# Stated queue orders for ScalarE and VectorE, and four block-product pairs instead of three in three input projections, in a one-core transformer layer

## Chip, cores and metric

The kernel runs on one core of a Trainium2 chip. The metric is the device time of one execution in microseconds (us); the median of the runs is compared. TensorE (PE) multiplies, VectorE (DVE) and ScalarE (ACT) prepare weights and evacuate results, GpSimd (POOL) issues a few accumulating transfers, SyncE (SP) issues the weight loads.

## The reference

One layer of a hybrid decoder, sequence 256, width 2048, all in fp32:

```python
x = x + 0.5 * swiglu(rmsnorm(x), w_gate1, w_up1, w_down1)     # FFN 1, hidden width 5632
h = rmsnorm(x)
q, k, v, mq, mk, mv, mo, mi, mf = split(h @ w_in)             # one input projection, 7176 columns
y_a = diff_attention(q, k, v)                                  # 4 heads
y_b = mlstm(silu(conv(mq, mk)), mv, mi, mf) * sigmoid(mo)      # 4 heads
x = x + concat(y_a, y_b) @ w_out
x = x + 0.5 * swiglu(rmsnorm(x), w_gate2, w_up2, w_down2)     # FFN 2
out = rmsnorm(x)
```

## The kernel before

**Products.** The 256 rows of x are two halves of 128; an output chunk is 512 columns (`CW`) and one half, one accumulator bank. Each fp32 weight tile is split into a high part (`wh`, a ScalarE copy, L116) and a low remainder (`wl`, a VectorE subtraction, L117); the activations are held in the same form (`xt`, `xs`). A product is then three matmuls of 128x512: high by high (L146), low of x by high (L147), high of x by low (L149, issued after the others of its unit). A unit is two K tiles of 128.

**Block products.** `Paired` computes two output chunks (columns of `wa` and of `wb`) at once. For the first `ns` of the pairs of K tiles it uses 7 block products instead of 8 (21 matmuls instead of 24 for such a pair); the rest is done as plain units. `first()` loads a pair of both weights (`raw`), forms weight sums on VectorE (L388 `sums<-raw`, L390 `raw<-sums,raw`), splits sums and weights (`halves_of`), and accumulates p5, p7 (`p57`) and p1, p6 (`p16`); after `p16` a GpSimd transfer adds one block of `raw` to another (L409, `raw<-raw`). `combine()` merges the banks: u is copied from p1 (ACT L434), u += p6 (DVE L435), p7 += u (L436), u3 copied from p7 (ACT L437), p6 = p5 - u3 (L438), p5 -= u (L439). `second()` adds to p1, p7, p5 the products of the bare weights (`bare`, which needs the transfer of L409), of the upper right block (`upper`), and the plain units of `wa`; `third()` adds the plain units of `wb`.

**Stages.** `Chain.run` interleaves `first()` of one `Paired` with `third()` of the one before. An FFN runs 11 gate and up pairs with `ns` = 4 of 8 (`NP`), in groups of 3, 3, 3, 2, each group followed by its share of the two down projections with `ns` = 3, 3, 3, 1 (`NP_DOWN`); the last, with `ns` = 1, ends an FFN. The mixer's five input projections use `ns` = 3 (`NP_MIX`), the out projection 2. At the start of FFN 1 `load_xt` loads and splits x, and `sum_xt` makes the sum form of a pair of x (`xg`, `xsum`, `xs`).

**What sets the order.** Each engine runs its own queue in order. The program is a list of tile operations with priorities (`high_priority`): weight loads, sums and splits are put 400 places ahead of where they stand (`AHEAD`), evacuations under `soon()` 440. A scheduler turns this into the queues. Buffers that bound how far loads and splits run ahead: `raw` 4, `rawp` and `sums` together 5, `wh`/`wl` 4 pairs. SP issues the weight loads in order, each when its buffer is free.

## Time and profile before

| | |
|---|---|
| time, median of 3 runs (lowest to highest) | 1796.76 us (1793.56 to 1799.55) |
| profiled execution: its own time | 1798.07 us |
| its span | 1796.4 us |
| mean granted TensorE clock | 0.997 |
| PE busy | 1773.1 us (99%), 8033 instructions |
| DVE busy | 1566.1 us (87%) |
| ACT busy | 1163.8 us (65%) |
| POOL busy | 176.7 us (10%) |

The span is the time from the first to the last recorded work; the execution's own time lies 1.67 us above it. Busy is the sum of an engine's instruction times without overlaps; a wait is the idle time ahead of an instruction, with the event that ended it.

### The profile page before, as it was taken

The numbers are of one execution on the slowest core, as the hardware profiler recorded it, in microseconds if no ns is written. First come the engines' busy times: TensorE is split into PE (matmuls) and PEld (weight loads), VectorE is DVE, ScalarE is ACT, GpSimd is POOL, SyncE is SP. The second block draws the span as 40 slices with busy tenths as digits, with TensorE's granted clock in tenths as the row PEclk, the third lists the DMA queues.
The fourth block names the chain that finished last, engine by engine and source line by source line (L and its number), as shares of the span: only waits on it lengthen the run. The fifth ranks groups of instructions, "written<-read, shape, count | busy, mean of one in ns | idle before, by whom it ended". The sixth has DMA issues, their size and how long they took to land.

```text
span 1796.4 us, 23431 instructions
## 1 busy us (share of the span) xinstructions
PE 1773.1 (99%) x8033; PEld 1463.6 (81%) x8033; DVE 1566.1 (87%) x1895; ACT 1163.8 (65%) x1512; POOL 176.7 (10%) x220
## 2 busy tenths in 40 slices
PE   9999999999999999999999999999999999999998
PEld 6788888887888878987888888888888888888886
DVE  6988899988998877796787988999899988998886
ACT  6666666666666656676566766666666666666664
POOL 0001100111002100000000000001100111002100
PEclk9999999999999999999999999999999999999999
DMA  9777877887788863665656665778877788778864
GB/s 340 220 226 223 239 230 231 258 237 223 218 261 235 257 236 122 209 215 196 196 191 197 192 194 165 220 240 249 233 243 232 249 236 243 211 254 239 262 193 152
DMA packets 124649, 402.76 MB, mean 224 GB/s; under 512 B 14001, under 2 KB 14513, under 8 KB 124273
## 3 DMA queue, kind: packets, MB, share of 16 engines
q1 hardware_dynamic: 96192, 349.35, 56.6%
q0 software_dynamic: 27328, 49.82, 16.5%
q10 hardware_dynamic: 1008, 2.09, 0.3%
q8 instruction: 63, 1.03, 0.2%
q14 instruction: 58, 0.47, 0.1%
HBM read 349.56 MB, written 2.10 MB: 196 GB/s over the span
## 4 chain that ended last, share of the span: by engine, by line
PE 86%; DMA 5%; issue 4%; DVE 4%; ACT 1%; SPq 0%; POOL 0%; DVEq 0%; POOLq 0%; ACTq 0%
PE acc L146 28%; PE acc L149 27%; PE acc L147 27%; DVE wl L117 2%; DMA raw<-in_wu_dram 2%; DMA rawp<-in_wu_dram 2%; PE tr L307 1%; ACT wh L116 1%; DVE sums L388 1%; DMA raw<-raw 0%; PE tr L250 0%; PE sc L946 0%; SPq L173 0%; PE num L897 0%; PE tr L689 0%
## 5 line engine op out<-in xcount | busy, mean ns | idle before, releaser
L116 ACT CAST wh<-raw 128x1024 fp32r<-128x1024 f32 (+3 forms) x448 | 402.0, 906 | 282.6 <-PE acc L147 180.4
L146 PE MATMUL acc<-wh,xt 128*128 128x512 f32 (+3 forms) x1444 | 559.8, 389 | 3.1 <-ACT wh L116 3.0
L147 PE MATMUL acc<-wh,xt 128*128 128x512 f32 (+3 forms) x1444 | 557.0, 387 | 0.0
L117 DVE TENSOR_TENSOR wl<-raw,wh 128x1024 fp32r<-128x1024 f32 (+3 forms) x448 | 459.7, 1039 | 86.2 <-ACT wh L116 83.2
L116 ACT CAST wh<-rawp 128x1024 fp32r<-128x1024 f32 (+1 forms) x358 | 372.7, 1044 | 156.0 <-PE acc L147 133.3
L117 DVE TENSOR_TENSOR wl<-rawp,wh 128x1024 fp32r<-128x1024 f32 (+1 forms) x358 | 430.9, 1207 | 44.9 <-ACT wh L116 41.6
L146 PE MATMUL acc<-wh,xs 128*128 128x512 f32 (+2 forms) x1071 | 420.2, 393 | 6.7 <-ACT wh L116 2.9
L147 PE MATMUL acc<-wh,xs 128*128 128x512 f32 (+2 forms) x1071 | 414.8, 388 | 0.0
L149 PE MATMUL acc<-wl,xt 128*128 128x512 f32 (+3 forms) x1444 | 398.5, 386 | 0.4 <-DVE wl L117 0.4
L149 PE MATMUL acc<-wl,xs 128*128 128x512 f32 (+2 forms) x1071 | 335.9, 389 | 2.7 <-DVE wl L117 2.5
L146 PEld LDWEIGHTS acc<-wh,xt 128*128 128x128 f32 x1444 | 271.5, 188 | 60.6 <-ACT wh L116 5.8
L147 PEld LDWEIGHTS acc<-wh,xt 128*128 128x128 f32 x1444 | 271.6, 188 | 54.0
L149 PEld LDWEIGHTS acc<-wl,xt 128*128 128x128 f32 x1444 | 269.7, 188 | 54.7 <-DVE wl L117 0.8
L146 PEld LDWEIGHTS acc<-wh,xs 128*128 128x128 f32 x1071 | 201.5, 188 | 49.0 <-ACT wh L116 3.7
L149 PEld LDWEIGHTS acc<-wl,xs 128*128 128x128 f32 x1071 | 200.1, 188 | 47.3 <-DVE wl L117 6.9
L409 POOL DMA_DIRECT2D raw<-raw x141 | 121.5, 863 | 1187.8 <-DVE wl L117 852.4
L147 PEld LDWEIGHTS acc<-wh,xs 128*128 128x128 f32 x1071 | 201.5, 188 | 39.4 <-DVE xs L112 0.4
L388 DVE TENSOR_TENSOR sums<-raw 128x1024 f32<-128x1024 f32 x141 | 171.8, 1219 | 43.7 <-DMA raw<-in_wu_dram 38.9
L116 ACT CAST wh<-sums 128x1024 fp32r<-128x1024 f32 x141 | 148.5, 1053 | 83.7 <-PE acc L147 62.6
L117 DVE TENSOR_TENSOR wl<-sums,wh 128x1024 fp32r<-128x1024 f32 x141 | 171.8, 1219 | 12.5 <-ACT wh L116 10.1
L390 DVE TENSOR_TENSOR raw<-sums,raw 128x512 f32<-128x512 f32 x141 | 96.3, 683 | 0.8
L293 POOL DMA_DIRECT2D xres<-part x48 | 44.4, 1002 | 265.6 <-ACT part L292 264.4
(199 smaller groups left out, 804.4 us busy)
## 6 DMA issues: line engine op xcount, KB each, us to landing
rawp<-in_wd_dram SPq DMA_DIRECT2D x96, 512.0 KB, 5.6
rawp<-in_wu_dram SPq DMA_DIRECT2D x94, 512.0 KB, 7.5
raw<-in_wg_dram SPq DMA_DIRECT2D x89, 512.0 KB, 7.1
rawp<-in_wg_dram SPq DMA_DIRECT2D x86, 512.0 KB, 6.0
raw<-in_wu_dram SPq DMA_DIRECT2D x82, 512.0 KB, 7.8
raw<-in_wd_dram SPq DMA_DIRECT2D x80, 512.0 KB, 6.2
raw<-raw POOLq DMA_DIRECT2D x141, 256.0 KB, 6.2
rawp<-in_win_dram SPq DMA_DIRECT2D x50, 512.0 KB, 4.9
```

The lines of the kernel that those rows point to most:

```text
L116: nc.scalar.copy(hi, src)
L117: nc.vector.tensor_tensor(out=lo, in0=src, in1=hi.bitcast(F32), op=ALU.subtract)
L146: nc.tensor.matmul(acc, lh, rh, start=first, stop=False, skip_group_check=on)
L147: nc.tensor.matmul(acc, ll, rh, start=False, stop=False, skip_group_check=on)
L149: nc.tensor.matmul(acc, lh, rl, start=False, stop=last, skip_group_check=on)
L293: nc.gpsimd.dma_start(xres[:, hb, c * CW:(c + 1) * CW], t, accum_op=ALU.add)
L307: nc.tensor.transpose(tr[:, i, hb * P:(hb + 1) * P], hs[hb][:, k * P:(k + 1) * P], ident)
L388: nc.vector.tensor_tensor(out=sums[j], in0=raw[:, 0:4:3, :], in1=raw[:, 2:3, :].to_broadcast([P, 2, CW]), op=ALU.add)
L390: nc.vector.tensor_tensor(out=raw[:, 2, :], in0=sums[j][:, 0, :], in1=raw[:, 3, :], op=ALU.add)
L409: nc.gpsimd.dma_start(raw[:, 2, :], raw[:, 1, :], accum_op=ALU.add)
```

## The change

Five things are changed. The middle three of the five input projections use 4 pairs in block products instead of 3 (`NPS_MIX`), and the sum form of x is made for 4 pairs there. `after(late, early)` states an order between two instructions of one engine without a semaphore: evacuations (`add_part`, `gate`, `gated`, the copies and additions of `combine`) are stated ahead of weight splits that come 4 or more splits later (`SLACK`), and a sum (L388, now L413) behind the VectorE split that lies 4 back (`SUMS`). `combine` is cut in two: u and u += p6 right behind the last `p16`, the rest (`combine_rest`) at the end of `first()`. Where `ns == 1`, the plain unit comes before the block products, and their split behind the copy of u3. At the start, two pairs of x get their sum form in `load_xt`, and the explicit call in `ffn` is gone.

```diff
-NP_MIX = 3
+NP_MIX = 4
+NPS_MIX = (3,4,4,4,3)
...
+SLACK = 4
+SUMS = 4
...
     def split(src, hi, lo):
-        nc.scalar.copy(hi, src)
-        nc.vector.tensor_tensor(out=lo, in0=src, in1=hi.bitcast(F32), op=ALU.subtract)
+        return (nc.scalar.copy(hi, src),
+                nc.vector.tensor_tensor(out=lo, in0=src, in1=hi.bitcast(F32), op=ALU.subtract))
+    splits, queued = [], ([], [])
+    def after(late, early):
+        tc.add_manual_dep(late.ins, early.ins.name,
+                          mybir.DependencyInfo(mybir.DependencyClass.NoSync, mybir.DependencyReason.DATA),
+                          reason="order")
+    def ahead_of_splits(i, ins):
+        queued[i].append((len(splits), ins))
+    def split_weights(src, hi, lo):
+        made = split(src, hi, lo)
+        for late, q in zip(made, queued):
+            while q and len(splits) >= q[0][0] + SLACK:
+                after(late, q.pop(0)[1])
+        return made
...
         with soon():
-            nc.scalar.activation(s, src, AF.Silu, scale=r)
+            ahead_of_splits(0, nc.scalar.activation(s, src, AF.Silu, scale=r))
...
-                    nc.vector.tensor_tensor(out=sums[j], in0=raw[:, 0:4:3, :],
-                                            in1=raw[:, 2:3, :].to_broadcast([P, 2, CW]), op=ALU.add)
+                    made = nc.vector.tensor_tensor(out=sums[j], in0=raw[:, 0:4:3, :],
+                                                   in1=raw[:, 2:3, :].to_broadcast([P, 2, CW]), op=ALU.add)
+                    if len(splits) >= SUMS:
+                        after(made, splits[-SUMS][1])
...
             p16(0)
+            if last == 0:
+                self.combine()
...
                 p16(j)
+                if j == last:
+                    self.combine()
...
                     p57(j)
+            self.combine_rest()
             yield
...
         def combine(self):
+            self.u = wk("u")
             with soon():
+                ahead_of_splits(0, nc.scalar.copy(self.u, self.p1))
+                ahead_of_splits(1, nc.vector.tensor_tensor(out=self.u, in0=self.p6, in1=self.u, op=ALU.add))
+        def combine_rest(self):
+            u, u3 = self.u, wk("u3")
+            p5, p6, p7 = self.p5, self.p6, self.p7
+            with soon():
+                ahead_of_splits(1, nc.vector.tensor_tensor(out=p7, in0=p7, in1=u, op=ALU.add))
+                self.copied = nc.scalar.copy(u3, p7)
+                ahead_of_splits(0, self.copied)
                 nc.vector.tensor_tensor(out=p6, in0=p5, in1=u3, op=ALU.subtract)
                 nc.vector.tensor_tensor(out=p5, in0=p5, in1=u, op=ALU.subtract)
...
             def bare(j):
...
-                    split(self.raws[j][:, 1:3, :], *t)
+                    splits.append(split_weights(self.raws[j][:, 1:3, :], *t))
+                    if self.ns == 1:
+                        after(splits[-1][0], self.copied)
...
-                if i < self.ns:
-                    bare(i)
-                    if i % 2 or i == self.ns - 1:
-                        upper(i - i % 2)
+                def blocks():
+                    if i < self.ns:
+                        bare(i)
+                        if i % 2 or i == self.ns - 1:
+                            upper(i - i % 2)
+                if self.ns > 1:
+                    blocks()
                 if i < len(self.rest):
...
+                if self.ns == 1:
+                    blocks()
...
-            p.combine()
             self.end()
...
-                    first[1]()
                     chain.put(stream, NP, functools.partial(end, au))
...
-        if u == KD // UK - 1:
+        if u >= KD // UK - NP_FIRST:
             sum_xt()
...
-    def both(c):
-        return Paired(xp2, win[c], win[c + 1], KD, NP_MIX)
+    def both(c, ns):
+        return Paired(xp2, win[c], win[c + 1], KD, ns)
```

The queues are shown at three places. A number behind a name tells buffers apart. First, VectorE at the start of the fifth gate and up pair of FFN 1 (174 to 202 us of the trace), before: `sums_1752` is the first weight sum there, `wl_1766` the sixth split behind it.

```order
L388 TENSOR_TENSOR sums_1752<-raw_1749 128x1024
L117 TENSOR_TENSOR wl_1697<-rawp_1694,wh_1696 128x1024
L390 TENSOR_TENSOR raw_1749<-sums_1752,raw_1749 128x512
L388 TENSOR_TENSOR sums_1797<-raw_1794 128x1024
L117 TENSOR_TENSOR wl_1729<-sums_1725,wh_1728 128x1024
L117 TENSOR_TENSOR wl_1739<-raw_1722,wh_1738 128x1024
L117 TENSOR_TENSOR wl_1756<-sums_1752,wh_1755 128x1024
L390 TENSOR_TENSOR raw_1794<-sums_1797,raw_1794 128x512
L388 TENSOR_TENSOR sums_1824<-raw_1821 128x1024
L117 TENSOR_TENSOR wl_1766<-raw_1749,wh_1765 128x1024
```

And with the change (L413 is L388 of before, L417 is L390, L120 is L117):

```order
L413 TENSOR_TENSOR sums_1752<-raw_1749 128x1024
L120 TENSOR_TENSOR wl_1697<-rawp_1694,wh_1696 128x1024
L417 TENSOR_TENSOR raw_1749<-sums_1752,raw_1749 128x512
L120 TENSOR_TENSOR wl_1729<-sums_1725,wh_1728 128x1024
L120 TENSOR_TENSOR wl_1739<-raw_1722,wh_1738 128x1024
L120 TENSOR_TENSOR wl_1756<-sums_1752,wh_1755 128x1024
L413 TENSOR_TENSOR sums_1797<-raw_1794 128x1024
L120 TENSOR_TENSOR wl_1766<-raw_1749,wh_1765 128x1024
L417 TENSOR_TENSOR raw_1794<-sums_1797,raw_1794 128x512
L120 TENSOR_TENSOR wl_1779<-rawp_1776,wh_1778 128x1024
```

The sum `sums_1797` has moved from ahead of three splits to behind them, and `sums_1824` from ahead of `wl_1766` to behind it, with its own addition (L390, L417).

Second, ScalarE at the first down projection with `ns == 1` (655 to 671 us), before; `raw_5603` is the pair of the block products, `rawp_5729` the plain unit, `u_5702` and `u_1171_5703` the copies of p1 and p7:

```order
L116 CAST wh_5686<-rawp_5684 128x1024
L116 CAST wh_5712<-raw_5603 128x1024
L116 CAST wh_5722<-raw_5603 128x512
L434 COPY u_5702<-acc_5599 128x512
L116 CAST wh_5731<-rawp_5729 128x1024
L437 COPY u_1171_5703<-acc_5601 128x512
L116 CAST wh_5765<-rawp_5763 128x1024
```

And with the change (L119 is L116, L466 is L434, L474 is L437; `rawp_5712` is the plain unit, `u_5666` and `u_1165_5669` the copies):

```order
L119 CAST wh_5694<-rawp_5692 128x1024
L119 CAST wh_5714<-rawp_5712 128x1024
L466 COPY u_5666<-acc_5599 128x512
L474 COPY u_1165_5669<-acc_5601 128x512
L119 CAST wh_5730<-raw_5603 128x1024
L119 CAST wh_5740<-raw_5603 128x512
L119 CAST wh_5765<-rawp_5763 128x1024
```

The plain unit's copy and the two copies of p1 and p7 have moved ahead of the copies of `raw_5603`.

Third, ScalarE at the start of FFN 1, before; `wh_149` is the first weight tile, in two halves, `xs_132` and `xs_139` the first two K pairs of x:

```order
L116 CAST wh_149<-raw_145 128x512
L111 ACTIVATE xs_132<-xraw_130,prm 128x256 x2
L111 ACTIVATE xs_139<-xraw_130,prm 128x256
L116 CAST wh_149<-raw_145 128x512
L111 ACTIVATE xs_139<-xraw_130,prm 128x256
L116 CAST wh_167<-raw_145 128x1024
```

And with the change (L114 is L111, L369 is L344):

```order
L119 CAST wh_149<-raw_145 128x512
L114 ACTIVATE xs_132<-xraw_130,prm 128x256
L369 ACTIVATE xg_301<-xraw_130,prm 128x256 x2
L114 ACTIVATE xs_139<-xraw_130,prm 128x256
L119 CAST wh_149<-raw_145 128x512
L114 ACTIVATE xs_139<-xraw_130,prm 128x256
L114 ACTIVATE xs_132<-xraw_130,prm 128x256
L119 CAST wh_167<-raw_145 128x1024
```

One slice of `xs_132` has moved behind the second half of `wh_149` and the slice of `xs_139`, and the gained copy `xg_301` of a second pair has come in.

## Rows read from the trace of the kernel before

**Rows 1.** The page of the profiled execution: the span, and the busy time of each engine with its share and instructions.

```profile
span 1796.4 us, 23431 instructions
...
PE 1773.1 (99%) x8033; PEld 1463.6 (81%) x8033; DVE 1566.1 (87%) x1895; ACT 1163.8 (65%) x1512; POOL 176.7 (10%) x220
```

**Rows 2.** TensorE's waits over the whole span for weight tiles: instruction and tile, what it waited for, us in total, times, longest.

```profile
PE acc L146 <- ACT wh L116: 5.9, 7, 2.5
PE acc L149 <- DVE wl L117: 2.9, 7, 0.6
```

**Rows 3.** The chain of waits: start in us, us, what. One unstalled group of four matmuls, and a transfer in the gate and up products of FFN 1.

```profile
65.48 0.91 PE acc L149 x4
...
269.57 7.73 DMA rawp<-in_wu_dram
```

**Rows 4.** Busy time by stretch: the stretch, its length, busy us of PE, PEld, DVE, ACT, POOL (instructions), granted clock of TensorE, share of the DMA engines, GB/s. FFN 1 without its start and end, the end of FFN 1, and the mixer.

```profile
60.00:660.00 600.00, 596.46 (x2663) 492.04 (x2662) 540.45 (x594) 385.16 (x453) 68.21 (x79) 1.00 0.79 236
660.00:700.00 40.00, 36.23 (x159) 28.60 (x158) 28.14 (x38) 21.48 (x34) 1.44 (x2) 0.96 0.62 199
700.00:1090.00 390.00, 389.92 (x1891) 327.46 (x1891) 323.93 (x484) 259.38 (x411) 24.62 (x33) 1.00 0.60 189
```

**Rows 5.** VectorE's waits over the whole span, the one of the weight sums.

```profile
DVE sums L388 <- DMA raw<-in_wu_dram: 38.9, 22, 3.8
```

**Rows 6.** VectorE in order of time at the start of a gate and up pass of FFN 1: start us, busy us, line, operation, tile; in brackets the idle time before it and what ended it.

```profile
190.74 1.23 DVE L388 TENSOR_TENSOR sums<-raw 128x1024 f32<-128x1024 f32 x1 [3.06 <-DMA raw<-in_wu_dram]
...
193.62 1.22 DVE L388 TENSOR_TENSOR sums<-raw 128x1024 f32<-128x1024 f32 x1
...
198.16 0.68 DVE L390 TENSOR_TENSOR raw<-sums,raw 128x512 f32<-128x512 f32 x1
198.77 1.21 DVE L388 TENSOR_TENSOR sums<-raw 128x1024 f32<-128x1024 f32 x1
199.90 1.21 DVE L117 TENSOR_TENSOR wl<-raw,wh 128x1024 fp32r<-128x1024 f32 x1
```

**Rows 7.** TensorE in order of time at the same place.

```profile
200.19 0.39 PE L147 MATMUL acc<-wh,xs 128*128 128x512 f32 x1
201.17 0.73 PE L149 MATMUL acc<-wl,xs 128*128 128x512 f32 x2 [0.59 <-DVE wl L117]
201.74 0.39 PE L146 MATMUL acc<-wh,xt 128*128 128x512 f32 x1
```

**Rows 8.** TensorE in order of time at the first of the last two down projections of FFN 1 (`ns == 1`): the last products of p1 and p6 (two matmuls in one row), then the block products and the plain unit.

```profile
661.58 0.62 PE L149 MATMUL acc<-wl,xs 128*128 128x512 f32 x2
...
667.70 0.39 PE L147 MATMUL acc<-wh,xs 128*128 128x512 f32 x1
669.93 0.50 PE L146 MATMUL acc<-wh,xs 128*128 128x512 f32 x1 [1.85 <-ACT u L437]
...
672.30 0.67 PE L146 MATMUL acc<-wh,xs 128*128 128x512 f32 x1 [1.17 <-DVE acc L439]
...
676.51 0.62 PE L149 MATMUL acc<-wl,xt 128*128 128x512 f32 x2
```

**Rows 9.** ScalarE in order of time at that place.

```profile
665.01 1.57 ACT L116 CAST wh<-raw 128x1024 fp32r<-128x1024 f32 x2 [6.71 <-PE acc L149]
666.49 0.58 ACT L434 COPY u<-acc 128x512 f32<-128x512 f32 x1
...
669.30 0.59 ACT L437 COPY u<-acc 128x512 f32<-128x512 f32 x1 [1.28 <-DVE acc L436]
```

**Rows 10.** SyncE's issue of the two loads of the down projection of which the first is the plain unit of [rows 8]; and the page's row on such loads (count, KB, median us from issue to landing).

```profile
650.11 2.14 SPq L173 DMA_DIRECT2D rawp<-in_wd_dram  x2
...
rawp<-in_wd_dram SPq DMA_DIRECT2D x96, 512.0 KB, 5.6
```

**Rows 11.** TensorE before the second of these projections.

```profile
696.37 1.29 PE L250 MATMUL tr<-ident,xres 128*128 128x128 f32 x7 [0.24 <-DVE xres L298]
698.09 0.50 PE L146 MATMUL acc<-wh,xs 128*128 128x512 f32 x1 [0.43 <-ACT u L434]
```

**Rows 12.** ScalarE at the start of FFN 1.

```profile
9.45 0.62 ACT L116 CAST wh<-raw 128x512 fp32r<-128x512 f32 x1 [2.31 <-DMA raw<-in_wg_dram]
9.97 0.50 ACT L111 ACTIVATE xs<-xraw,prm 128x256 fp32r<-128x256 f32 x1
```

**Rows 13.** TensorE at the same place, and where the up projection of the first chunk begins to share the engine.

```profile
10.12 0.67 PE L146 MATMUL acc<-wh,xs 128*128 128x512 f32 x1 [2.45 <-ACT wh L116]
...
46.29 0.50 PE L146 MATMUL acc<-wh,xt 128*128 128x512 f32 x1 [1.06 <-ACT wh L116]
...
51.11 0.50 PE L146 MATMUL acc<-wh,xs 128*128 128x512 f32 x1 [0.44 <-ACT wh L116]
```

**Rows 14.** ScalarE just ahead of 46.29 us, and VectorE just ahead of 51.11 us.

```profile
45.20 1.04 ACT L116 CAST wh<-rawp 128x1024 fp32r<-128x1024 f32 x1
...
49.17 0.69 DVE L390 TENSOR_TENSOR raw<-sums,raw 128x512 f32<-128x512 f32 x1
```

**Rows 15.** TensorE at the stall behind the transfer of [rows 3].

```profile
278.48 0.50 PE L146 MATMUL acc<-wh,xt 128*128 128x512 f32 x1 [0.85 <-ACT wh L116]
```

**Rows 16.** Groups of VectorE's instructions with the shapes kept apart: count, busy us, mean ns of one, idle time before.

```profile
L388 DVE TENSOR_TENSOR sums<-raw 128x1024 f32<-128x1024 f32 x141 | 171.8, 1219 | 43.7 <-DMA raw<-in_wu_dram 38.9 <-DMA raw<-in_win_dram 2.2 <-DMA raw<-in_wd_dram 1.7
...
L435 DVE TENSOR_TENSOR u<-acc,u 128x512 f32<-128x512 f32 x44 | 30.1, 683 | 1.1 <-ACT u L434 1.1
```

More of the change, by code (lines that the diff above doesn't have):

```diff
@@ L137, in split_w @@
             for n in pieces:
-                split(raw[:, o:o + n, :], hi[:, o:o + n, :], lo[:, o:o + n, :])
+                made = split_weights(raw[:, o:o + n, :], hi[:, o:o + n, :], lo[:, o:o + n, :])
                 o += n
+        splits.append(made)
         return hi, lo
@@ L291, in add_part @@
         with soon():
-            nc.scalar.activation(t, acc, AF.Copy, scale=0.5)
+            ahead_of_splits(0, nc.scalar.activation(t, acc, AF.Copy, scale=0.5))
         nc.gpsimd.dma_start(xres[:, hb, c * CW:(c + 1) * CW], t, accum_op=ALU.add)
@@ L324, in gate @@
         with soon():
-            nc.scalar.activation(s, src, AF.Silu, scale=r)
+            ahead_of_splits(0, nc.scalar.activation(s, src, AF.Silu, scale=r))
         return s
     def gated(src, r, s):
-        nc.vector.scalar_tensor_tensor(s, src, r, s, op0=ALU.mult, op1=ALU.mult)
+        ahead_of_splits(1, nc.vector.scalar_tensor_tensor(s, src, r, s, op0=ALU.mult, op1=ALU.mult))
         return s
@@ L394, in halves_of @@
                     t = pair_tiles(wsp, "w", [P, 2, CW])
-                    split(src, *t)
+                    splits.append(split_weights(src, *t))
                 return t
@@ L430, in combine @@
         def combine(self):
-            u, u3 = wk("u"), wk("u3")
-            p1, p5, p6, p7 = self.p1, self.p5, self.p6, self.p7
+            self.u = wk("u")
             with soon():
-                nc.scalar.copy(u, p1)
-                nc.vector.tensor_tensor(out=u, in0=p6, in1=u, op=ALU.add)
-                nc.vector.tensor_tensor(out=p7, in0=p7, in1=u, op=ALU.add)
-                nc.scalar.copy(u3, p7)
+                ahead_of_splits(0, nc.scalar.copy(self.u, self.p1))
[7 more added lines that the diff above has]
+                ahead_of_splits(0, self.copied)
                 nc.vector.tensor_tensor(out=p6, in0=p5, in1=u3, op=ALU.subtract)
@@ L466, in upper @@
                     for i, j in enumerate(js):
-                        split(self.raws[j][:, 3, :], t[0][:, i, :], t[1][:, i, :])
+                        made = split_weights(self.raws[j][:, 3, :], t[0][:, i, :], t[1][:, i, :])
+                splits.append(made)
                 mms([self.job(n12, j, S4, t, i, False, False, True) for i, j in enumerate(js)])
@@ L858, in tile_trunk_layer @@
     qT, kT = [], []
-    chain.run(both(2), to_T(qT), to_T(qT))
+    chain.run(both(2, NPS_MIX[0]), to_T(qT), to_T(qT))
     sws = []
@@ L904, in tile_trunk_layer @@
     by_head(scores)
-    chain.run(both(0), functools.partial(take_mv, 0), functools.partial(take_mv, 1))
+    chain.run(both(0, NPS_MIX[1]), functools.partial(take_mv, 0), functools.partial(take_mv, 1))
     by_head(numerators)
-    chain.run(both(4), to_T(kT), to_T(kT))
+    chain.run(both(4, NPS_MIX[2]), to_T(kT), to_T(kT))
     enm = late["enm"]
@@ L1030, in tile_trunk_layer @@
     by_head(attend)
-    chain.run(both(6), take_av, take_av)
-    chain.run(both(8), functools.partial(gate_out, 0), functools.partial(gate_out, 1))
+    chain.run(both(6, NPS_MIX[3]), take_av, take_av)
+    chain.run(both(8, NPS_MIX[4]), functools.partial(gate_out, 0), functools.partial(gate_out, 1))
     pending[:0] = later
```

## Prediction

> **What bounds the kernel now.** I read the page first. PE is busy 1773.1 of 1796.4 us [rows 1]: whatever the change does on ScalarE and VectorE can reach the time only through the 23.3 us in which PE is idle, through the slow restart behind each such gap, and through the number of matmuls. Then the pace: four unstalled 128x512 matmuls take 0.91 us in the chain of waits [rows 3], 0.227 us each; the 0.39 us of a single row [rows 7] is a pipelined duration and no price. Then the price of a stall. At 200.19 us a matmul starts, and the next at 201.17 [rows 7]: 0.98 instead of 0.227, so 0.75 late, of which the row shows 0.59 as idle; the two behind it take 0.57 instead of 0.455. In all 0.87 us for 0.59 of idle time, so I add 0.28 us to each idle time shown.
>
> Where the idle time lies comes from the waits and the stretches. PE waited for a split of VectorE (`wl`) 7 times, 2.9 us in all, and for a copy of ScalarE (`wh`) 7 times, 5.9 us [rows 2]. In 60 to 660 us PE idles 3.5 of 600 us, at the end of FFN 1 3.8 of 40, in the mixer 0.1 of 390 [rows 4]. VectorE's longest waits that are not for ScalarE are those of the weight sums for the `wu` load: 22 times, 38.9 us [rows 5]. So there are four kinds of places: VectorE late in the FFNs, ScalarE late behind loads, the end of FFN 1, the start.
>
> **The change part by part.** The sum is made against the profiled execution, 1798.07 us; the median of the runs shown is 1.31 us lower.
>
> *A. Sums behind splits, in the FFNs.* At 190.74 us a sum has waited 3.06 us for its load; the sum at 193.62 and the one at 198.77 with an addition (198.16) stand ahead of the split that starts at 199.90 [rows 6], and PE's stall at 201.17 waits for this split, which ends at 201.11. By the order of the changed kernel one sum and one addition have gone behind this split. From starts in [rows 6] a sum takes 199.90 - 198.77 = 1.13 us of the queue and an addition 198.77 - 198.16 = 0.61, so the split ends 1.74 us earlier, at 199.4. PE wants it at 200.19 + 0.227 = 200.42. The stall goes, with 1 us to spare. The sum moved latest (193.62) then ends at about 198.2; ScalarE's copy of it and VectorE's split stand two splits further on, so what is late next is that copy, with some 2 us to spare. The order shows such a move, of one sum or more, at each of the seven waits. They cost 2.9 + 7 x 0.28 = 4.9 us. Bounds 0 and -4.9; I take **-4.5**, as the spare time where I followed it is larger than the stall.
>
> *B. ScalarE late behind loads.* The stall at 278.48 (0.85 us [rows 15]) follows a load of 7.73 us [rows 3]. SP's order and ScalarE's there do not change. **0**.
>
> *C. The two down projections at FFN 1's end.* Here `second()` starts with the block products, whose copy waits on ScalarE 6.71 us until 665.01, with the copy of u behind it (666.49) and that of u3 at 669.30 [rows 9], though p1 and p6 had their last matmuls at 661.58 [rows 8]. PE loses between 667.70 and 669.93 2.23 - 0.23 = 2.0 us; from 669.93 to 672.30 it does four matmuls, 2.37 - 0.91 = 1.46 lost; from 672.30 to 676.51 eleven, 4.21 - 2.50 = 1.71 lost [rows 8]. The last is no wait: behind the idle time eight of these matmuls run at about twice 0.227 us, in a stretch with a mean granted clock of 0.96 [rows 4], so at the lower of the clock's two levels, 1.2 instead of 2.4 GHz. Together 5.2 us. With the change the plain unit comes first, its 12 matmuls (2.7 us) from 667.47 on. Its load is issued at 650.11 and such a load lands after 5.6 us in the middle [rows 10], so its copy can run before 660. u follows at about 662.4, then with 0.5 to 0.7 us a step ([rows 9], and 0.683 us for an addition [rows 16]) u += p6, p7 += u, u3 and the last two: done at about 666, before 667.47. The bare block's copy starts, as now, at 665.01 or behind u3, and its products are wanted only at 667.47 + 2.72 = 670.2; copy and split (1.04 + 1.2 us) end by 667.5. Second projection: 0.24 and 0.43 us of idle time [rows 11], with two restarts 1.2 us, of the same cause. Bounds: -1 (if the copies of u still come last and only the two plain matmul groups cover them) and -6.4; I take **-6.4**. FFN 2's end has the same code, and little idle time there; 0.
>
> *D. The start.* Loss: the second slice of the first x pair now stands behind the second half of the first weight (9.45 us) and another slice (9.97) [rows 12]. PE's second start, 10.12 now [rows 13], follows it: 9.97 + 0.4 + 0.5 = 10.9, so +0.8. Gain: the stall at 46.29 (1.06 + 0.28) has its copy start at 45.20 [rows 13, 14], behind gained copies and splits of x that move to 7 us or behind it; and that at 51.11 (0.44 + 0.28) is behind an addition at 49.17 that moves ahead of two splits. Bounds +0.8 and -1.3; I take **-1.2**.
>
> *E. Fewer matmuls.* Three projections get one pair more in block form, 21 instead of 24 matmuls: 9 x 0.227 = **-2.0**. PE does not wait in the mixer [rows 4], so this counts in full.
>
> *F. What these pairs cost.* Each adds a sum (1.22) and an addition (0.68 [rows 16]), and its splits are 3.5 tiles instead of 2, 1.8 us more: 3.7 us of VectorE, 11 in all, and one more sum form of x, 1.2 us. VectorE idles 390 - 323.9 = 66 us there, DMA stands at 0.60 and not 0.79 [rows 4]. What hides it is that slack; if it is not there at the start of a pass, it costs a stall like that of 278.48, 0.85 + 0.28 = 1.13 us, in each of the three. Bounds 0 and +3.4; I take **+1.0**, nearer to none, since VectorE keeps 17% free against 10% in the FFN.
>
> The evacuation orders themselves (`SLACK`) I cost at nothing: the order shows ScalarE's queue in the FFN passes almost as before; the cover is 1 to 2 us by which splits run ahead of PE, and the price without it is the second rival's.
>
> Sum: -4.5 + 0 - 6.4 - 1.2 - 2.0 + 1.0 = -13.1, so 1785.0; with about half of the 1.31 us to the median, **1784.5 us**.
>
> **The rivals.** (1) *The wait moves from the sum to the load.* In A the splits reach the front sooner, and the next sums come later; if ScalarE's copies of the sums, or a slot of `raw` freed later, then end last, A gives nothing, and D and F cancel: -6.4 - 2.0 = -8.4, 1789.5. For it speak the 38.9 us that sums wait for loads [rows 5] and a DMA share of 0.79 [rows 4]; against it the 2 us of spare time at 198.
>
> (2) *The other side: a stated evacuation holds the splits.* A copy or addition that must stand ahead of splits waits for PE's last product of its bank; splits behind it, which PE needs, wait with it. The place is each `combine`, 44 in the kernel [rows 16]. It undoes the sum from 13.1 / 44 = 0.30 us on each, about one restart, and makes the kernel measurably slower from (13.1 + 5.4) / 44 = 0.42 us; at 0.59 + 0.28, the size of the stall of [rows 7], it gives +38 - 13 and 1823; at half that 1804. For it: VectorE has a split waiting behind such a step as it is, 1.1 us over all of L435 [rows 16], so steps do wait. Against it: that is 1.1 us in 44 of them. The Trainium skill, "Perfetto Trace Analysis", section "Tensor Engine Instruction (MATMUL, LD_WEIGHTS)", says that ScalarE and VectorE keep strict order while TensorE can pull weight loads ahead; by this rule nothing behind a waiting evacuation could slip past it, and the change would lose wherever splits have no lead. The trace agrees that the order is kept: the copy of u at 666.49 stood behind the copy that waited 6.71 us, with its input long done [rows 8, 9].
>
> (3) *The mixer becomes VectorE's.* With 4 pairs the mixer looks like an FFN pass; each of the three projections stalls at its bound, and if A gives nothing, as in rival 1, and C only its lower bound, -1 - 2.0 - 1.2 + 3.4 = -0.8 is left: no change, about 1796.5. For it: FFN passes with 4 pairs have PE idle 3.5 us in 600. Against it: VectorE's 66 us and the DMA share there [rows 4].
>
> (4) *More than forecast*: the loads of B start sooner too, since splits free `raw` earlier: the four waits for `wh` in B go as well. They are the 5.9 us of [rows 2] less the 2.45, 1.06 and 0.44 us of [rows 13], 1.95, and 4 x 0.28, 3.1 us in all: 1781.4.
>
> **How the numbers follow.** Forecast 0.60 (its own range 1781 to 1788), rival 1 0.20, rival 2 0.06, rival 3 0.08, rival 4 0.06. 0.3% (5.4 us) is about what a measurement of this kernel tells from no change, so faster means below 1791.4. Faster: 0.60 + 0.15 + 0.06 = 0.81; same: 0.05 of rival 1, 0.08, 0.01 of rival 2: 0.14; slower 0.05. The range takes in rivals 1 and 4 and the bounds of A, D and F: 1778 to 1793.
>
> **What would show it.** C: no idle time of PE at 660 to 700 us, and a granted clock of 1.00 there. A: PE's waits for `wl` in the FFNs gone or below 1 us in all, while sums still wait for loads. B: the waits for `wh` behind loads still there. D: PE's second start near 10.9, and no idle time at 44 to 52. E and F: 9 matmuls fewer, and idle time of PE in the mixer below 1 us. The prediction is wrong if PE's idle time in the mixer rises over 3 us, if new waits for `wh<-sums` stand where those for `wl` were, or if PE waits for an accumulator that an evacuation frees late.

## Result and the profile after

The changed kernel takes 1786.1 us (median of 6 runs, 1782.96 to 1787.17), the kernel before beside it 1797.57, so 11.5 us less; the ratio of the two is 0.9935, 95% interval 0.9922 to 0.9948. The forecast was 1784.5. The profiled execution has a span of 1784.2 us, 12.2 us less.

The page after, beside [rows 1]:

```profile
span 1784.2 us, 23416 instructions
...
PE 1767.8 (99%) x8024; PEld 1462.9 (82%) x8024; DVE 1576.2 (88%) x1910; ACT 1166.6 (65%) x1520; POOL 176.7 (10%) x223
```

PE idles 16.4 us instead of 23.3, and does nine matmuls less. Its waits, beside [rows 2]:

```profile
PE acc L171 <- ACT xs L114: 2.9, 2, 2.5
PE acc L171 <- ACT wh L119: 2.7, 6, 0.7
```

The waits for `wl` are gone, and those for `wh` have fallen from 5.9 to 2.7 us; but PE now waits for the split of x at the start. By stretch, beside [rows 4]:

```profile
60.00:660.00 600.00, 598.50 (x2676) 494.94 (x2675) 540.27 (x595) 385.90 (x455) 67.30 (x79) 1.00 0.79 238
660.00:700.00 40.00, 39.99 (x188) 32.85 (x187) 37.12 (x54) 29.56 (x47) 1.42 (x2) 1.00 0.52 173
700.00:1090.00 390.00, 389.92 (x1893) 327.98 (x1892) 334.56 (x494) 265.27 (x416) 29.17 (x38) 1.00 0.65 197
```

At 660 to 700 us nothing is idle, and the granted clock is 1.00; in FFN 1 1.5 us is idle instead of 3.5; in the mixer 0.1 as before, with 10.6 us more of VectorE.

Idle time alone misses the pace. To place the 12.2 us, I took transposes that both programs do, and compared their starts. Two of them, the first behind FFN 1's end and the first behind the out projection, in the trace of before:

```profile
723.06 1.03 PE L250 MATMUL tr<-ident,xres 128*128 128x128 f32 x8
...
1112.95 0.82 PE L250 MATMUL tr<-ident,xres 128*128 128x128 f32 x6
```

and after:

```profile
712.69 0.49 PE L275 MATMUL tr<-ident,xres 128*128 128x128 f32 x3
...
1100.49 0.71 PE L275 MATMUL tr<-ident,xres 128*128 128x128 f32 x5
```

From one to the other took 389.89 us before and 387.80 after. Five such marks (before, they start at 66.22, 638.00, 723.06, 1112.95 and 1751.58 us) give six stages, for every kernel that ran but the two with a sixth buffer; each number is the length of a stage less that of before, in us:

| kernel | start | FFN 1 | its end | mixer, out proj. | FFN 2 | its end | span |
|---|---|---|---|---|---|---|---|
| changed | -0.9 | -3.0 | -6.5 | -2.1 | -0.1 | +0.3 | -12.2 |
| end_old | -2.6 | -2.4 | -0.1 | -2.1 | -0.5 | +2.0 | -5.7 |
| end_copies | -2.2 | -2.7 | -3.5 | -2.2 | -0.4 | +0.6 | -10.3 |
| end_only | +0.2 | -0.9 | -3.3 | 0.0 | -1.0 | -0.1 | -5.1 |
| sums_free | -2.5 | 0.0 | -6.7 | +1.7 | -0.9 | -0.1 | -8.5 |
| sums2 | -1.2 | +21.3 | -5.1 | +3.7 | +34.5 | -0.1 | +53.1 |
| mix3 | -2.2 | -2.1 | -6.6 | -0.1 | +0.1 | +0.3 | -10.6 |
| mix4 | -1.6 | -3.1 | -6.7 | +4.6 | -0.7 | +0.4 | -7.1 |
| start_old | -1.7 | -2.8 | -6.6 | -2.2 | +0.4 | +0.3 | -12.6 |
| comb_old | -0.6 | -3.2 | -6.6 | -2.1 | -1.6 | +0.4 | -13.7 |
| slack1 | +2.7 | +22.9 | +0.1 | +0.4 | +33.5 | +1.7 | +61.3 |

Each row is one execution. Starts with one and the same order there (changed, end_old, end_copies, mix3, mix4) lie 1.7 us apart, and FFN 2 of kernels that differ elsewhere (changed, end_old, end_copies, mix3, start_old) 0.9. A difference under about 1 us in a cell says nothing, and in the start none under 2.

The place of part A after the change, VectorE, beside [rows 6]:

```profile
188.88 1.23 DVE L413 TENSOR_TENSOR sums<-raw 128x1024 f32<-128x1024 f32 x1 [1.56 <-DMA raw<-in_wu_dram]
...
195.17 1.22 DVE L413 TENSOR_TENSOR sums<-raw 128x1024 f32<-128x1024 f32 x1
196.30 1.22 DVE L120 TENSOR_TENSOR wl<-raw,wh 128x1024 fp32r<-128x1024 f32 x1
197.44 0.68 DVE L417 TENSOR_TENSOR raw<-sums,raw 128x512 f32<-128x512 f32 x1
```

and PE, beside [rows 7]:

```profile
199.25 0.39 PE L172 MATMUL acc<-wh,xs 128*128 128x512 f32 x1
199.48 0.62 PE L174 MATMUL acc<-wl,xs 128*128 128x512 f32 x2
```

The split that PE waits for (196.30) now has one sum ahead of it where two and an addition stood; it ends at 197.5, and PE takes it at 199.48 without idle time.

The end of FFN 1, ScalarE, beside [rows 9]:

```profile
656.10 1.05 ACT L119 CAST wh<-rawp 128x1024 fp32r<-128x1024 f32 x1 [1.67 <-PE acc L172]
658.14 0.59 ACT L466 COPY u<-acc 128x512 f32<-128x512 f32 x1 [0.98 <-PE acc L174]
660.22 0.59 ACT L474 COPY u<-acc 128x512 f32<-128x512 f32 x1 [1.49 <-DVE acc L473]
661.36 1.57 ACT L119 CAST wh<-raw 128x1024 fp32r<-128x1024 f32 x2 [0.56 <-DMA raw<-raw]
```

The plain unit's copy runs at 656.10, u and u3 at 658.14 and 660.22; the copy of the block pair comes last and waits 0.56 us, now with the GpSimd transfer named as releaser.

### The profile page after: what moved, and what is told of

It is laid out like the page before. It is cut to its first block, busy times and chain, and to the rows that moved or that the text cites. A ratio compares the mean times of both kernels' runs of the same rounds, so it can differ in the third digit from the quotient of the medians.

```text
span 1784.2 us, 23416 instructions
## 1 busy us (share of the span) xinstructions
PE 1767.8 (99%) x8024; PEld 1462.9 (82%) x8024; DVE 1576.2 (88%) x1910; ACT 1166.6 (65%) x1520; POOL 176.7 (10%) x223
## 3 DMA queue, kind: packets, MB, share of 16 engines
q10 hardware_dynamic: 1008, 2.09, 0.3%
## 4 chain that ended last, share of the span: by engine, by line
PE 95%; DMA 2%; ACT 1%; issue 1%; DVE 0%; SPq 0%; POOLq 0%; POOL 0%; ACTq 0%; DVEq 0%
PE acc L171 31%; PE acc L172 30%; PE acc L174 30%; DMA rawp<-in_wu_dram 2%; PE tr L332 1%; ACT wh L119 1%; PE tr L275 0%; DMA raw<-in_wg_dram 0%; PE sc L992 0%; PE num L943 0%; DVE wl L120 0%; SPq L198 0%; PE tr L1031 0%; PE tr L735 0%; PE rr L913 0%
## 5 line engine op out<-in xcount | busy, mean ns | idle before, releaser
L119 ACT CAST wh<-raw 128x1024 fp32r<-128x1024 f32 (+3 forms) x457 | 409.6, 906 | 244.9 <-PE acc L172 167.4
L171 PE MATMUL acc<-wh,xt 128*128 128x512 f32 (+2 forms) x1392 | 539.7, 388 | 2.3 <-ACT wh L119 2.3
L172 PE MATMUL acc<-wh,xt 128*128 128x512 f32 (+2 forms) x1392 | 538.1, 387 | 0.0
L120 DVE TENSOR_TENSOR wl<-raw,wh 128x1024 fp32r<-128x1024 f32 (+3 forms) x457 | 469.9, 1040 | 60.7 <-ACT wh L119 56.8
L120 DVE TENSOR_TENSOR wl<-rawp,wh 128x1024 fp32r<-128x1024 f32 (+1 forms) x352 | 424.2, 1208 | 67.9 <-ACT wh L119 64.6
L119 ACT CAST wh<-rawp 128x1024 fp32r<-128x1024 f32 (+1 forms) x352 | 366.4, 1043 | 167.5 <-PE acc L172 128.2
L171 PE MATMUL acc<-wh,xs 128*128 128x512 f32 (+2 forms) x1120 | 439.8, 394 | 3.3 <-ACT xs L114 2.9
L172 PE MATMUL acc<-wh,xs 128*128 128x512 f32 (+2 forms) x1120 | 433.8, 388 | 0.1
L174 PE MATMUL acc<-wl,xt 128*128 128x512 f32 (+2 forms) x1392 | 384.9, 387 | 0.0
L174 PE MATMUL acc<-wl,xs 128*128 128x512 f32 (+2 forms) x1120 | 348.3, 389 | 0.1
L171 PEld LDWEIGHTS acc<-wh,xt 128*128 128x128 f32 x1392 | 261.3, 188 | 57.3 <-ACT wh L119 4.4
L172 PEld LDWEIGHTS acc<-wh,xt 128*128 128x128 f32 x1392 | 261.6, 188 | 52.3 <-DVE xt L120 0.3
L174 PEld LDWEIGHTS acc<-wl,xt 128*128 128x128 f32 x1392 | 260.5, 188 | 52.3
L171 PEld LDWEIGHTS acc<-wh,xs 128*128 128x128 f32 x1120 | 211.1, 189 | 46.8 <-ACT xs L114 4.2
L174 PEld LDWEIGHTS acc<-wl,xs 128*128 128x128 f32 x1120 | 209.1, 188 | 44.8 <-DVE wl L120 2.7
L172 PEld LDWEIGHTS acc<-wh,xs 128*128 128x128 f32 x1120 | 211.2, 189 | 41.3 <-DVE xs L115 0.8
L119 ACT CAST wh<-sums 128x1024 fp32r<-128x1024 f32 x144 | 151.5, 1052 | 98.2 <-PE acc L172 48.9
L413 DVE TENSOR_TENSOR sums<-raw 128x1024 f32<-128x1024 f32 x144 | 175.0, 1218 | 25.8 <-DMA raw<-in_wu_dram 25.1
L120 DVE TENSOR_TENSOR wl<-sums,wh 128x1024 fp32r<-128x1024 f32 x144 | 175.7, 1220 | 10.8 <-ACT wh L119 9.5
L417 DVE TENSOR_TENSOR raw<-sums,raw 128x512 f32<-128x512 f32 x144 | 98.6, 685 | 0.8
```

Source lines behind the costliest of these rows:

```text
L119: return (nc.scalar.copy(hi, src), nc.vector.tensor_tensor(out=lo, in0=src, in1=hi.bitcast(F32), op=ALU.subtract))
L120: nc.vector.tensor_tensor(out=lo, in0=src, in1=hi.bitcast(F32), op=ALU.subtract))
L171: nc.tensor.matmul(acc, lh, rh, start=first, stop=False, skip_group_check=on)
L172: nc.tensor.matmul(acc, ll, rh, start=False, stop=False, skip_group_check=on)
L174: nc.tensor.matmul(acc, lh, rl, start=False, stop=last, skip_group_check=on)
L413: made = nc.vector.tensor_tensor(out=sums[j], in0=raw[:, 0:4:3, :], in1=raw[:, 2:3, :].to_broadcast([P, 2, CW]), op=ALU.add)
```

## Experiments

**end_old.** The order at the FFNs' end undone.

```diff
-                    if self.ns == 1:
-                        after(splits[-1][0], self.copied)
...
-                if self.ns > 1:
-                    blocks()
+                blocks()
...
-                if self.ns == 1:
-                    blocks()
```

> The changed kernel with only the order at the end of the FFNs undone: the block products stand before the plain unit again, and their split is not stated behind the copy of u3. Theory (the 6.4 us at FFN 1's end come from this order): the loss between 655 and 725 us of the trace returns, about 6.5 us, so 1786.1 + 6.5 = 1792.6 us; everything ahead of 655 us stays as in the changed kernel. Rival (the cut of combine or the other stated orders removed that loss): within 1 us of 1786.1.

1790.93 us, ratio 0.9968 (0.9956 to 0.9981); the stage lost 6.4 of 6.5 us. The medians are 4.8 us apart, less than the 6.5 expected and far from the rival's 1 us. PE at the place:

```profile
666.27 0.79 PE L171 MATMUL acc<-wh,xs 128*128 128x512 f32 x1 [3.08 <-ACT u L474]
```

u3 is late again, 3.08 us at one place, and the granted clock is 0.50 at 666 to 672 us. The order there is the cause. The stage at FFN 2's end loses 1.7 us too, by a like wait at 1762.97 us (1.01) that the kernel before doesn't have.

**end_copies.** Blocks first, but behind u3: of the edit above, only the stated order is kept.

```diff
-                if self.ns > 1:
-                    blocks()
+                blocks()
...
-                if self.ns == 1:
-                    blocks()
```

> The changed kernel with the block products before the plain unit at the end of the FFNs, but their split still stated behind the copy of u3. It asks which half of that edit pays. Theory (what cost PE was the copies of u and u3 standing behind a copy that waits for the GpSimd transfer): with the copies ahead, the banks are ready, and PE waits only for the bare block itself. In the changed kernel its copy ran at 661.36 and its split ended at 663.66; PE comes there at about 663.6, so at most 0.7 us is lost, and the time is 1786.1 to 1787. Rival (the plain unit is needed as cover for the transfer): 2 us or more of idle time at that place and a stretch at the lower clock behind it, 1789 or more.

1787.88 us, ratio 0.9951 (0.9938 to 0.9963). The stage gives 3.5 us instead of 6.5:

```profile
663.59 0.50 PE L171 MATMUL acc<-wh,xs 128*128 128x512 f32 x1 [0.81 <-ACT wh L119]
...
666.77 0.50 PE L174 MATMUL acc<-wl,xs 128*128 128x512 f32 x1 [0.72 <-DVE wl L120]
```

The banks are ready, but PE waits for the bare block's copy, for which ScalarE stood 2.68 us until the GpSimd transfer had landed, and then for the split of the upper one: 1.53 us and two restarts. Neither expectation holds as it stands: more than 0.7 us is lost, but the idle time at the place is under the rival's 2 us, the granted clock at 660 to 700 us is 1.00, and the time lies between the two. By the stage table the copies' order is worth 3.4 us (end_old to end_copies) and the plain unit as cover for the transfer 3.0 (end_copies to changed), of which these two waits explain 2.1.

**end_only.** The same edit as in the change, plain unit first and the split behind u3, alone in the kernel before.

```diff
...
-                nc.scalar.copy(u3, p7)
+                self.copied = nc.scalar.copy(u3, p7)
...
+                    if self.ns == 1:
+                        after(made, self.copied)
...
+                if self.ns > 1:
+                    blocks()
...
+                if self.ns == 1:
+                    blocks()
```

> The kernel before with the order at the end of the FFNs alone changed: plain unit first, the split of the block products behind the copy of u3; 3 pairs in the mixer, no order of the sums, combine in one piece. Theory (the parts add up: -6.4 us there by the forecast, 6.5 by the trace of the changed kernel, and nothing elsewhere): 6.4 us under the kernel before, ratio 0.9964, the stalls for wl in the FFNs and those at 46 and 51 us as before. Rival (part of the 6.5 us needs the cut of combine): 3 to 5 us under it.

1793.0 us, ratio 0.9971 (0.9959 to 0.9982). The stage gives 3.3 us, half:

```profile
673.37 0.50 PE L155 MATMUL acc<-wl,xs 128*128 128x512 f32 x1 [0.32 <-DVE wl L117]
...
692.50 0.50 PE L152 MATMUL acc<-wh,xt 128*128 128x512 f32 x1 [0.43 <-ACT u L440]
...
695.05 0.51 PE L152 MATMUL acc<-wh,xt 128*128 128x512 f32 x1 [0.89 <-ACT u L443]
```

At the first projection no wait for u or u3 is left. At the second, u is late as it was before, and u3 now too. The three waits shown, one of 0.24 us for `xres` and their restarts make 3.0 us in the stage; before, the second projection alone lost 1.2. The time, 4.5 us below the kernel before, is the rival's, but its reason isn't. What is missing is not the cut of `combine` but its place: before, `combine` was called behind the last step of the other stream; comb_old (below), with combine in one piece at the end of `first()`, ahead of that step, has the full 6.6 us. Comb_old differs from end_only in other parts too, but sums_free, mix3 and start_old, each without one of these, keep 6.6 us or more.

**sums_free.** No stated order for the sums.

```diff
-                    if len(splits) >= SUMS:
-                        after(made, splits[-SUMS][1])
```

> The changed kernel without the stated order of the weight sums (SUMS); VectorE's queue at the place shown (190 to 202 us) is then as before. Theory (this order alone took away the 2.9 us of stalls for wl in FFN 1, and it also made the new stalls of FFN 2 at 1209.6 us): waits of PE for wl return, some 2.1 us of idle time in FFN 1 and 0.8 in FFN 2, the stall at 1209.6 goes; 1786.1 + 2.9 + 0 = 1789.0. Rival (the cut of combine did it): 1786, no waits for wl in FFN 1.

1789.63 us, ratio 0.9967 (0.9954 to 0.9979).

```profile
PE acc L174 <- DVE wl L120: 2.3, 5, 0.7
...
PE acc L171 <- DVE den L369: 1.8, 1, 1.8
PE acc L171 <- ACT aexp L369: 1.5, 1, 1.5
```

FFN 1's gain is gone to the last tenth (0.0 instead of -3.0), with 2.0 of these 2.3 us of waits there. The surprise is the mixer, 3.8 us longer: a division of the mLSTM (`den`) and an exponential of the attention (`aexp`) come late, 1.76 and 1.47 us. With 4 pairs and free sums, VectorE and ScalarE get to them too late. With 3 pairs and free sums (end_only, 0.0) the mixer loses nothing, nor with 4 pairs and the order (changed): the order of the sums is what lets the fourth pair in at no cost.

**sums2.** A sum behind the split 2 back, in the kernel with combine in one piece.

```diff
-SUMS = 4
+SUMS = 2
```

> The changed kernel with combine in one piece, and a weight sum stated behind the split 2 back instead of 4 back. At the place shown (190 to 202 us) the queue is the same as with 4. Theory (a sum needs to get behind one split at each of the seven places, and there is a microsecond to spare): no more than 0.5 us from the kernel with 4, 1786. Rival (sums that come earlier put themselves ahead of evacuations in the mixer again, as without the order): idle time of PE at 880 to 945 us and 1788 or more.

1850.56 us, ratio 1.0296 (1.0282 to 1.031). The expected time failed, and the rival has the direction of the time but not the reason: a smaller number puts a sum later, not earlier. VectorE:

```profile
294.51 0.69 DVE L417 TENSOR_TENSOR raw<-sums,raw 128x512 f32<-128x512 f32 x1
```

ScalarE:

```profile
295.36 1.04 ACT L119 CAST wh<-raw 128x1024 fp32r<-128x1024 f32 x1 [3.46 <-issue]
```

PE:

```profile
296.46 0.50 PE L171 MATMUL acc<-wh,xs 128*128 128x512 f32 x1 [2.09 <-ACT wh L119]
```

The addition of the sum (294.51) ends at 295.2, ScalarE's copy of its result starts at 295.36, PE waits 2.09 us. Of PE's 27 waits for `wh` in this trace (33.5 us), 17 (23.2 us) are for such a copy, which starts within 0.2 us behind an addition's end. This is the mechanism of the forecast's first rival: once the sum is late, `wh` of its raw pair is late. 4 lies between two costs, 3.5 us with none and 64 with 2; 3 and 5 were not run.

**mix3.** 3 pairs in all five projections.

```diff
-NP_MIX = 4
-NPS_MIX = (3,4,4,4,3)
+NP_MIX = 3
+NPS_MIX = (3,3,3,3,3)
```

> The changed kernel with 3 pairs in block form in all five input projections, as before. Theory (nine matmuls at 0.227 us, and no cost on VectorE or ScalarE): 1786.1 + 2.0 = 1788.1, and the difference arises between 800 and 1000 us of the trace. Rival (the pairs cost the 1.0 us that was forecast): 1787.1. A third: the added sum form of x at 700 us costs time that was hidden in the gain at FFN 1's end; then the stretch from 660 to 725 us gets shorter.

1787.08 us, ratio 0.9946 (0.9933 to 0.9958). The mixer is 2.0 us longer than in the changed kernel (-0.1 against -2.1), the nine matmuls at 0.227 us, and no other stage is shorter beyond its spread. At 700 to 1090 us PE idles 0.1 us with the pairs and without: they cost nothing. The times themselves, 1.0 us apart, can't tell 1 from 2.

**mix4.** 4 pairs in all five.

```diff
-NPS_MIX = (3,4,4,4,3)
+NPS_MIX = (4,4,4,4,4)
```

> The changed kernel with 4 pairs in block form in all five input projections. Theory (a pair more costs nothing while VectorE has slack): six matmuls fewer, 1786.1 - 1.4 = 1784.7. Rival (the first projection starts while x is still being transposed and has no slack, the last is followed by the out projection): new idle time of PE at 720 to 740 or at 1000 to 1090 us, 1 to 2 us each, 1786 to 1788.

1791.01 us, ratio 0.9961 (0.9948 to 0.9973), with six matmuls less again.

```profile
PE acc L171 <- ACT wh L119: 4.6, 7, 1.3
...
PE tr L1031 <- ACT xg L369: 1.3, 2, 0.7
PE acc L171 <- ACT xs L119: 1.0, 1, 1.0
```

The mixer is 6.7 us longer than in the changed kernel. The longest new waits are those for `wh` at 791 and 806 us (1.06, 1.29), where `third()` of the first projection runs beside `first()` of the second, and those for the mixer's output, transposed for the out projection (`xg`), and for its split at 993 to 996 us (0.53, 0.74, 1.02). So a pair more in the first and the last projection isn't free, as the forecast feared in F for the other three; the change leaves these two alone. Which of the two pairs makes which wait was not run.

**start_old.** The start of FFN 1 as before.

```diff
+                    first[1]()
...
-        if u >= KD // UK - NP_FIRST:
+        if u == KD // UK - 1:
```

> The changed kernel with the start of FFN 1 as before: one pair's sum form in load_xt, the second by the explicit call. Theory (the start gives 0.9 to 2.6 us by the traces of the changed kernel and four variants that share its start, the spread coming from when the first weights land): the stalls at 46 and 51 us return, 2.1 us with their restarts, the long stretch at the lower clock at 12 to 16 us goes, 1.2 us; the time is 1786.1 + 1 = 1787. Rival (the start gives nothing that counts): 1786.1, with both stalls there. The forecast of the start was 1.2 us.

1787.01 us, ratio 0.9933 (0.992 to 0.9945), as the changed kernel. The stalls are back:

```profile
45.85 0.49 PE L174 MATMUL acc<-wl,xt 128*128 128x512 f32 x1 [0.49 <-DVE wl L120]
...
49.38 0.51 PE L171 MATMUL acc<-wh,xs 128*128 128x512 f32 x1 [0.95 <-ACT wh L119]
```

but the stage, -1.7, lies within the spread of the others. The start's gain isn't shown.

**slack1.** Evacuations ahead of all splits one or more behind them.

```diff
-SLACK = 4
+SLACK = 1
```

> The changed kernel with evacuations stated ahead of all splits that come one or more behind them (SLACK = 1 instead of 4). With 4 the stated order leaves the queues as they are without it. Theory (the second rival's mechanism: a waiting evacuation holds the splits that PE needs): PE waits for wh and wl behind copies of u or Silu, at many of the 44 places, 0.3 to 0.9 us each: 1795 to 1820. Rival (splits run so far ahead that the order is free): 1786 to 1788, waits as in the changed kernel.

1859.78 us, ratio 1.0343 (1.0328 to 1.0358). PE, then ScalarE:

```profile
PE acc L171 <- ACT wh L119: 41.3, 69, 3.3
```

```profile
ACT u L466 <- PE acc L174: 63.6, 41, 4.6
ACT sg L350 <- PE acc L174: 57.2, 40, 3.9
```

ScalarE stands 63.6 us before copies of u whose bank PE hasn't finished (2.7 us in the changed kernel) and 57.2 before Silu, and PE waits 41.3 us for copies of weights. One such place, ScalarE and PE:

```profile
134.22 0.69 ACT L350 ACTIVATE sg<-acc,rstd 128x512 f32<-128x512 f32 x1 [0.67 <-PE acc L174]
134.80 1.04 ACT L119 CAST wh<-rawp 128x1024 fp32r<-128x1024 f32 x1
```

```profile
135.89 0.50 PE L171 MATMUL acc<-wh,xt 128*128 128x512 f32 x1 [0.35 <-ACT wh L119]
```

The copy of the weights (134.80) starts right behind a Silu that had waited for PE, and PE waits for the copy. This is the second rival's mechanism, and it is real. 41 of the 69 waits are of this kind (the copy stands in an unbroken row behind an evacuation that waited), but only 14.0 of the 41.3 us; 38 of them stand behind `gate` or `add_part`, 3 at a `combine`, where the rival had put them all. In 19 others (11.4 us) the copy starts right behind the addition of a weight sum, as in sums2, and in 7 (11.9 us) it waits for a load; how far these follow from the held evacuations isn't shown. Together the stated order costs 74 us over the changed kernel. With 4 it isn't in force at all: the scheduled program is the same, instruction for instruction, with and without it.

**comb_old.** `combine` in one piece at the end of `first()`.

```diff
             p16(0)
-            if last == 0:
-                self.combine()
...
-                if j == last:
-                    self.combine()
...
+            self.combine()
             self.combine_rest()
```

> The changed kernel with combine in one piece at the end of first(), as before. Theory (where u is taken matters only where PE waits for a bank; outside the end of the FFNs it never did): 1786.1, within 1 us, with no new waits of PE for a bank. Rival (taking u early frees VectorE's queue in the FFN passes and keeps stalls away there): waits of PE for wl or for u in the FFNs, 1788 or more.

1786.07 us, ratio 0.9931 (0.9918 to 0.9943): the cut is worth nothing measurable.

```profile
PE acc L171 <- ACT wh L119: 1.9, 5, 0.7
```

Its FFN 2 is 1.5 us shorter in this one trace, and the new stall of the changed kernel (below) isn't in it; the times can't confirm that.

**rawp6 and rawp6w6.** comb_old with a sixth buffer for `rawp` and sums, and fewer work buffers.

```diff
-    work = ctx.enter_context(tc.tile_pool(name="work", bufs=8))
+    work = ctx.enter_context(tc.tile_pool(name="work", bufs=7))
...
-    wrp = ctx.enter_context(tc.tile_pool(name="wrp", bufs=5))
+    wrp = ctx.enter_context(tc.tile_pool(name="wrp", bufs=6))
```

> The changed kernel with combine in one piece (which by itself changed nothing measurable), 6 buffers instead of 5 for rawp and sums, and 7 instead of 8 work buffers to make room; the queues of PE, DVE, ACT and GpSimd are the same as without the two sizes. It asks what the remaining stalls of the FFNs wait for (PE for a wh whose load is late: 0.75, 0.53, 0.19, 0.07 and 0.20 us at 277, 465, 1160, 1347 and 1534 us, some 3 us with restarts). Theory (SP can issue the third load of the row only when a buffer is free): with one more it is issued and lands earlier, the five stalls go, -3 us, 1783. Rival (the transfers themselves are the limit, DMA at 0.79 there, or the sixth buffer only lets loads collide): the stalls stay, 1786.

1824.43 us, ratio 1.0151 (1.0137 to 1.0164), though PE waits less than ever. Its waits for `wh`, and the page:

```profile
PE acc L171 <- ACT wh L119: 0.7, 2, 0.4
```

```profile
PE 1808.7 (99%) x8024; PEld 1462.7 (80%) x8024; DVE 1583.2 (87%) x1910; ACT 1169.1 (64%) x1520; POOL 177.0 (10%) x223
```

PE is busy 41 us more with the same instructions. In the chain, four matmuls take

```profile
15.06 0.93 PE acc L174 x4
```

where the changed kernel has

```profile
64.56 0.91 PE acc L174 x4
```

Over the 512-column matmuls the mean distance of starts is 233.3 ns instead of 227, alike in every 100 us of the trace, at a granted clock of 0.997. The second run asked whether the place of the weight tiles does it:

```diff
-    work = ctx.enter_context(tc.tile_pool(name="work", bufs=7))
+    work = ctx.enter_context(tc.tile_pool(name="work", bufs=6))
```

> The kernel with 6 buffers for rawp and sums, but 6 work buffers instead of 7, so that the weight tiles wh and wl lie at the same place in SBUF as in the changed kernel (two work buffers of 2 KB less, one rawp buffer of 4 KB more; with 7 they lay 2 KB further on). It asks why with 7 every 512-column matmul took 233.3 ns instead of 227, and whether the sixth buffer pays. Theory (the place of the weight tiles made the matmuls slower, and the sixth buffer takes the late loads away): pitch back at 227 ns, no stall of PE behind a late load but the first, 1782 to 1784, if two work buffers less cost nothing. Rival (the pitch hangs on something else that the sixth buffer or the shorter work pool brings, or on the place of raw and rawp): 233 ns again, 1820 or more.

1824.92 us, ratio 1.0156 (1.0142 to 1.017), 233.3 ns again. So that place (as it follows from the pool sizes) isn't the cause, or not alone. Of the five late loads two stalls are left in both runs, but PE is 2.8% slower there and needs its loads later; what the sixth buffer gives stays open.

## Why the prediction was right, and where not

**C, the end of FFN 1: -6.4 forecast, -6.5 by the marks, 6.4 lost in end_old.** The largest term held, the 1.7 us at the lower clock included: without the idle time the granted clock stayed at 1.00. The step priced the edit as one. end_copies shows two halves, 3.4 us for the earlier copies of u and 3.0 for the plain unit as cover, and the step's working has both: the copies done before the plain unit begins, and the blocks wanted only behind it. What it passed over is the place of `combine`, without which the second projection loses again (end_only).

**A, sums behind splits: -4.5 forecast, -3.0 by the marks.** In FFN 1 the mechanism and the size are right (sums_free: 2.9 to 3.0 us): at the place followed, the split ends 8.6 us behind the start of the first sum, and the step had 199.4 - 190.74 = 8.7. In FFN 2 the 1.4 us there (of the 2.9 us of idle time, 0.8, with two restarts) didn't arrive: the stage is -0.1. The waits for `wl` are gone there too, but a new one for `wh` stands at 1209.56 us, as rival 1 had it. VectorE:

```profile
1204.21 1.22 DVE L413 TENSOR_TENSOR sums<-raw 128x1024 f32<-128x1024 f32 x1
...
1207.62 0.69 DVE L417 TENSOR_TENSOR raw<-sums,raw 128x512 f32<-128x512 f32 x1
1209.54 1.23 DVE L120 TENSOR_TENSOR wl<-raw,wh 128x1024 fp32r<-128x1024 f32 x1 [1.23 <-ACT wh L119]
```

ScalarE:

```profile
1200.85 1.05 ACT L119 CAST wh<-rawp 128x1024 fp32r<-128x1024 f32 x1 [5.11 <-DMA rawp<-in_wu_dram]
...
1208.46 1.05 ACT L119 CAST wh<-raw 128x1024 fp32r<-128x1024 f32 x1 [2.56 <-PE acc L174]
```

PE:

```profile
1209.56 0.50 PE L171 MATMUL acc<-wh,xs 128*128 128x512 f32 x1 [0.41 <-ACT wh L119]
```

ScalarE stands 5.11 us before a copy whose load hasn't landed; that holds the split behind it, and with it the sum (1204.21), so the addition (1207.62), the copy of its pair (1208.46) and the split (1209.54) come late: the mirror of A. The row of that copy names PE as what ended the wait, but this product had ended by 1207.8; the copy starts 0.15 us behind the addition's end (1208.31), as in sums2. This chain is read from the rows. Neither sums_free nor comb_old has a stall there, mix3 and start_old have it again (0.28 and 0.47 us), and end_old, end_copies and mix4, with the same order and cut, don't: it hangs on when the load lands, and no run changes this place alone. The stall and its restart make 0.7 of the 1.4 us; the rest is within the 0.9 us by which this stage varies. So the term was over-sized by some 1.5 us, by taking FFN 2 as FFN 1.

**E and F: -2.0 and +1.0 forecast, -2.1 together.** E is confirmed by mix3. F was mis-sized: in the three projections chosen the cost is nil, not 1.0; its upper bound, 3.4, was far exceeded in the two others (mix4: 6.7 us, although six matmuls are saved). What hid it wasn't VectorE's slack alone, as the step had it, but that with the order of the sums (sums_free).

**D, the start: -1.2 forecast, -0.9 in this trace, not measurable in time.** The loss had the right mechanism. ScalarE after, beside [rows 12], and PE, beside [rows 13]:

```profile
8.71 0.62 ACT L119 CAST wh<-raw 128x512 fp32r<-128x512 f32 x1 [0.54 <-DMA raw<-in_wg_dram]
9.23 0.91 ACT L114 ACTIVATE xs<-xraw,prm 128x256 fp32r<-128x256 f32 x2
```

```profile
10.19 1.22 PE L171 MATMUL acc<-wh,xs 128*128 128x512 f32 x2 [2.54 <-ACT xs L114]
...
15.05 0.63 PE L172 MATMUL acc<-wh,xs 128*128 128x512 f32 x1
```

From the copy's start to PE's start it takes 1.48 us instead of 0.67, as forecast 0.8 more; that PE started at 10.19 and not at 10.9 is due to a load 0.74 us earlier. Not forecast was that the lower clock then lasts to 16 us instead of 13.6, 1.2 us; but the runs don't show that the order does this: in mix3, with the same start, the granted clock is 1.00 from 14 us on, as before, against 0.71 at 14 to 18 us here. Both stalls at 46 and 51 us went.

**B: 0 forecast.** The stalls behind late loads are there: 276.46 (0.68), 464.71, 1159.87, 1348.39 and 1535.39 us. The evacuation orders, costed at nothing, are nothing: they change no queue.

In sum -13.1 was forecast and -12.2 measured in the span. That the two are so close is in part luck: A gave 1.5 us less than forecast, E and F 1.1 us more, and these cancel. Of the rivals, the first took a third of A, the second's mechanism shows with `SLACK` = 1, the third in the two projections that the change leaves alone; the late loads of the fourth stayed. The strict order of ScalarE and VectorE that the Trainium skill states ("Perfetto Trace Analysis", section "Tensor Engine Instruction (MATMUL, LD_WEIGHTS)") was weighed for the second rival. slack1 agrees with it: the copy at 134.80 us starts only behind the Silu that had waited.

## What to carry to other kernels

When the bound engine is 99% busy, list its few stalls, price each with its restart (here 0.28 us beside the idle time, and 1.7 us of lower clock behind the waits of 1.85 and 1.17 us), and ask for each what stands ahead of the late instruction in its queue that could stand behind it. An order between a producer and work of less haste has two sides: one place too early stalls the split, two too late stall the sum, and the distance has to be found by running it: here only 4, 2 and no order were run. A stated order that leaves every queue as it is can be seen from the queues alone, before anything is measured.
